# A Toeplitz form cut into 4 KB pieces, and a norm's channel factors moved from the weights to the rows

## The chip, the cores and the metric

One core of a Trainium2 chip runs the whole program in one launch. The metric is device time in microseconds (us); lower is better. The kernel before takes 1645.49 us, the median of three runs (1643.48, 1645.49, 1648.16). The engines are named as in the profile: PE is TensorE (PEld its weight loads), DVE is VectorE, ACT is ScalarE, POOL is GpSimd, SP is SyncE, which issues most of the transfers.

## The reference

Two residual layers over 512 tokens of 1024 channels, all in float32. The even layer mixes tokens with an RWKV-7 recurrence and pooling; the odd layer, where the change lies, with differential attention beside an S5 state-space layer. Both are followed by a mixture of experts (MoE).

```python
h = rms_norm(x, norm_mix_g[layer])          # x * rsqrt(mean(x*x) + eps) * g, g one factor per channel
u = h @ w_in
q, k, v, u_s5 = split(u, ...)               # 512 columns each
...
# S5: 32 groups of 16 channels, a complex diagonal state of 64 per group
bu = einsum('gpc,btgc->btgp', b_bar, uf)
_, states = associative_scan(combine, (lam_bar, bu))
y = einsum('gcp,btgp->btgc', c_mat, states).real + d_skip * uf
```

## The kernel before, in words

The program runs the even mixer, its MoE, the odd mixer and its MoE one after another. A scheduler orders each engine's instructions when the program is built; generators in the source (`run_all`) interleave what it gets. Each engine works its own list strictly in that order, so an instruction that waits holds everything behind it.

**Odd projections.** `odd_mixer` transposes x on PE into eight blocks of 128 channels (`pt`), and splits each into a rounded part and a remainder, `hhi` on ACT and `hlo` on DVE (lines 1817 to 1821). `project(c0, cols)` (line 1869) multiplies them by 512 columns of the weights. A weight ring holds pieces that SP loads; for every pair of channel blocks `split_gain` (line 156) makes `whi` on ACT and `wlo` on DVE, two instructions of 128x512 on each, since each block has its own column of channel factors `gain`. Then come 24 matmuls `pu` (four row blocks, two channel blocks, three products: lines 1883 to 1885), 96 in a unit of 512 columns. There are four units: the S5 input (`to_states`), then keys, queries and values (`to_attention`). After the key and the query unit a chain of ACT and DVE work normalises and rotates the heads (`us`, `rsq`, `sq`, `wk`, lines 1911 to 1936), and PE transposes each result (`ptq`, line 1941).

**The S5 layer** (`states()`, line 1967) works on 64 chunks of 8 tokens. `U` holds the input with 8 tokens times 16 channels on the 128 partitions. What follows, in order:

- `W` (POOL and DVE, lines 1983 to 1985) is transposed on PE (`pw`) to `Wt`, which takes a chunk into the state; `P7` holds the powers of the decay for it.
- `pk` (line 2002) makes the response of the layer, 128 numbers per row (8 lags times 16 channels), 16 rows per group; ACT copies it to `Ks` (line 2008). POOL's queue writes 112 zeros per row (line 1996) and then the 128 numbers (line 2017) to the DRAM scratch `Kd`, 240 numbers per row.
- `pj` (line 2031) takes the chunks into the state, and a scan with its rotations (lines 2037 to 2051) makes `XP`, on DVE and POOL.
- SP reads `Kd` back as `M` (lines 2053 to 2057), the lower triangular Toeplitz matrix of each group: eight transfers, one per token of a chunk, each to 16 partitions in runs of 512 bytes, each shifted by 16 numbers. `M` takes the memory of `Wt`, so the first transfer waits for the last `pj`.
- `pyy` (lines 2063 and 2067) adds `U` times `M` and `XP` times `Q`: 16 groups of matmuls, four of them to a bank, and ACT copies the bank out (line 2070).

PE's list mixes all this with the `pu` matmuls of the attention units. The next stage is attention with the gated unit of the S5 output; the MoE's weights are streamed behind it.

## Time and profile before

| | |
|---|---|
| median of three runs | 1645.49 us |
| the profiled execution | 1643.12 us |
| its span in the trace | 1641.4 us |
| PE busy | 1528.8 us, 93% of the span |
| DVE busy | 819.5 us, 50% |
| ACT busy | 447.9 us, 27% |
| POOL busy | 230.4 us, 14% |
| odd mixer before attention | about 868 to 1021 us of the span |

The shares are means over stages with different limits, so they tell where to look and not what a change is worth. The trace gives for each instruction its start and length, and in brackets the idle time of its engine ahead of it with what ended that. The span is 1.7 us shorter than the execution, and the profiled execution 2.4 us shorter than the median.

### The profile page before, as it was taken

Reading aid. Unit: us, or ns where it says so; the run is one execution under the profiler, and the core shown is the slowest. Engines: PE = TensorE matmul, PEld = TensorE weight load, DVE = VectorE, ACT = ScalarE, POOL = GpSimd, SP = SyncE. Lnnn points to the kernel's source line nnn. Section 1 sums busy time; section 2 is a strip of 40 time slices with the busy share of each in tenths; the row PEclk is TensorE's granted clock in tenths of the full one; section 3 lists DMA queues with packets and bytes.
Section 4 is the critical chain, followed back from the end, with each engine's and each line's share of the span. In section 5 each row is a group of like instructions: output and inputs, shape, how many; then the busy total and the mean of one; then the engine's idle time right before and its main releaser. Section 6 shows DMA issues by size and latency. Waiting matters only on the chain. (4 is left out here: it accounts for less than half of the span.)

```text
span 1641.4 us, 24906 instructions
## 1 busy us (share of the span) xinstructions
PE 1528.8 (93%) x9852; PEld 886.1 (54%) x9852; DVE 819.5 (50%) x1942; ACT 447.9 (27%) x1029; POOL 230.4 (14%) x268
## 2 busy tenths in 40 slices
PE   8998988999999999999998998799999999999997
PEld 6776666776444444433348775577544444433433
DVE  5577878776233333332764694764433333322323
ACT  5234434332212121111314533741021211211110
POOL 2342331200000000000211242501000000000000
PEclk9999999999999999999999999799999999999999
DMA  7210100177899999999992262209789999999996
GB/s 223 97 65 21 51 4 2 53 295 294 337 420 419 419 420 420 420 419 418 420 387 63 66 94 59 103 26 356 308 363 420 419 420 420 419 420 421 420 420 236
DMA packets 95564, 453.62 MB, mean 276 GB/s; under 512 B 12507, under 2 KB 30715, under 8 KB 49360
## 3 DMA queue, kind: packets, MB, share of 16 engines
q1 hardware_dynamic: 88144, 438.01, 67.9%
q0 software_dynamic: 5968, 13.58, 2.4%
q8 instruction: 80, 1.31, 0.3%
q10 hardware_dynamic: 1328, 0.36, 0.1%
q14 instruction: 44, 0.36, 0.1%
HBM read 452.91 MB, written 6.78 MB: 280 GB/s over the span
## 5 line engine op out<-in xcount | busy, mean ns | idle before, releaser
L1198 PE MATMUL pgu<-w,XT 128*64 128x512 f32 x1920 | 452.4, 596 | 22.3 <-DMA w<-in_moe_w_gate 19.1
L1198 PEld LDWEIGHTS pgu<-w,XT 128*64 128x64 f32 x1920 | 141.9, 137 | 312.3 <-issue 256.6
L1288 DVE TENSOR_TENSOR x<-pc,x 128x512 f32<-128x512 f32 x240 | 149.3, 682 | 163.6 <-PE pc L1198 163.6
L1198 PE MATMUL pd<-w,hTe 128*64 128x512 f32 x960 | 213.9, 598 | 0.6 <-ACT hTe L1336 0.6
L1327 DVE SCALAR_TENSOR_TENSOR hid<-hid,gs,pgu 128x512 f32<-128x512 f32 x32 | 23.9, 747 | 242.6 <-PE pgu L1198 234.9
L1095 POOL DMA_INDIRECT rows<-rows,idx x30 | 30.0, 999 | 759.6 <-DVE O L1215 590.3
L1198 PEld LDWEIGHTS pd<-w,hTe 128*64 128x64 f32 x960 | 66.6, 137 | 122.7 <-issue 112.9
L1256 ACT ACTIVATE XT<-pga,p_norm 128x128 f32<-128x128 f32 x240 | 68.3, 371 | 195.1 <-PE pga L1198 191.3
L1345 DVE TENSOR_TENSOR ylo<-pd,yhi 128x512 fp32r<-128x512 f32 (+1 forms) x68 | 44.8, 659 | 138.8 <-ACT yhi L1344 138.8
L1326 ACT ACTIVATE hid<-pgu,gs 128x512 f32<-128x512 f32 x32 | 22.0, 688 | 288.9 <-PE pgu L1198 288.9
L1198 PE MATMUL pc<-yhi,S 128*128 128x512 f32 x240 | 100.4, 418 | 0.0
L1198 PE MATMUL pc<-ylo,S 128*128 128x512 f32 x240 | 94.9, 395 | 0.0
L1344 ACT ACTIVATE yhi<-pd 128x512 fp32r<-128x512 f32 (+1 forms) x68 | 38.9, 572 | 170.9 <-PE pd L1198 153.4
L161 DVE SCALAR_TENSOR_TENSOR wlo<-w,p_norm,whi 128x512 fp32r<-128x512 f32 (+1 forms) x72 | 56.3, 813 | 44.9 <-ACT whi L160 44.9
L160 ACT ACTIVATE whi<-w,p_norm 128x512 fp32r<-128x512 f32 (+1 forms) x72 | 46.3, 692 | 77.8 <-PE pu L665 42.3
L1198 PEld LDWEIGHTS pc<-yhi,S 128*128 128x128 f32 x240 | 45.3, 189 | 34.1 <-issue 26.0
L664 PE MATMUL pu<-hhi,whi 128*128 128x512 f32 x144 | 58.6, 411 | 0.2 <-DVE u L672 0.2
L665 PE MATMUL pu<-hlo,whi 128*128 128x512 f32 x144 | 57.8, 401 | 0.0
L1884 PE MATMUL pu<-wlo,hhi 128*128 128x512 f32 x128 | 53.4, 419 | 3.4 <-DVE wlo L161 3.4
L666 PE MATMUL pu<-hhi,wlo 128*128 128x512 f32 x144 | 55.2, 402 | 0.0
L1883 PE MATMUL pu<-whi,hhi 128*128 128x512 f32 x128 | 51.0, 416 | 1.7 <-ACT us L1895 1.7
L1885 PE MATMUL pu<-whi,hlo 128*128 128x512 f32 x128 | 52.5, 416 | 0.0
(539 smaller groups left out, 2502.7 us busy)
## 6 DMA issues: line engine op xcount, KB each, us to landing
w<-in_moe_w_down SPq DMA_DIRECT2D x120, 1024.0 KB, 20.0
w<-in_moe_w_gate SPq DMA_DIRECT2D x120, 1024.0 KB, 20.0
w<-in_moe_w_up SPq DMA_DIRECT2D x120, 1024.0 KB, 20.2
w<-in_even_w_in SPq DMA_DIRECT2D x8, 1024.0 KB, 5.2
w<-in_moe_w_gate SPq DMA_DIRECT2D x16, 512.0 KB, 8.2
w<-in_moe_w_up SPq DMA_DIRECT2D x16, 512.0 KB, 9.6
w<-in_moe_w_down SPq DMA_DIRECT2D x16, 512.0 KB, 9.3
w<-in_odd_w_in SPq DMA_DIRECT2D x8, 1024.0 KB, 5.1
```

The lines of the kernel that those rows point to most:

```text
L160: nc.scalar.activation(hi[:, k, :], w[:, k, :], AF.Copy, scale=g[:, k:k + 1])
L161: nc.vector.scalar_tensor_tensor(lo[:, k, :], w[:, k, :], g[:, k:k + 1], r32(hi[:, k, :]), op0=OP.mult, op1=OP.subtract)
L664: nc.tensor.matmul(out[j], a, hhi[:, kt, :], start=kt == 0, stop=False)
L665: nc.tensor.matmul(out[j], a, hlo[:, kt, :], start=False, stop=False)
L666: nc.tensor.matmul(out[j], b, hhi[:, kt, :], start=False, stop=kt == KD - 1)
L1198: return self.K.tc.keep_in_program_order(op(*args, **kw))
L1256: nc.scalar.activation(self.XTs[j][:, k, :], p[:, i, :], AF.Copy, scale=B.gain[:, k:k + 1])
L1288: V.tensor_tensor(self.x[:, t, c], p, self.x[:, t, c], OP.add)
L1345: self.nc.vector.tensor_tensor(yl[:, c], p, r32(yh[:, c]), OP.subtract)
L1883: nc.tensor.matmul(out[j], a, whi[:, k, :], start=kt == 0, stop=False)
L1884: nc.tensor.matmul(out[j], a, wlo[:, k, :], start=False, stop=False)
L1885: nc.tensor.matmul(out[j], b, whi[:, k, :], start=False, stop=kt == KD - 1)
```

## The change

Three things change together.

1. `Kd` is laid out anew: the 32 groups split as 4 times 8, and the 8 lie innermost, so that a row has 240 entries of 8 numbers. `M` is then read by four transfers over all 128 partitions, each in one run of 4 KB per partition. For that the tokens of a chunk stand in reverse in `us` and `U`, and the powers `P7` with them. The zeros go out in eight stores in place of one, with the same 512 runs of 448 bytes. ACT writes `Ks` with a step of 8 numbers (32 bytes), and the `pyy` matmuls read `M` with that step.
2. The channel factors of the odd norm multiply the rows when `hhi` and `hlo` are made, and no longer the weights. The weights are split by `split`, one instruction of 128x1024 on each of ACT and DVE in place of two of 128x512.
3. The interleaving counts of `states()` change by one `yield`.

```diff
@@ -1804,7 +1804,8 @@
     lv = cp.tile([128, 6, 64], F32, name="lv")
     A.dma_start(lv.rearrange("p a b -> p (a b)"), I["lam"].to_broadcast([128, 384]))
     K.ocst = K.load(cp, "c_odd", ODD_CONST)
-    Kd = dram.tile([32, 16, 240], F32, name="Kd")
+
+    Kd = dram.tile([4, 16, 240, 8], F32, name="Kd")
     v = []
     qkT = [keep.tile([128, 4, T], F32, name=f"qkT{i}") for i in range(2)]
 
@@ -1818,7 +1819,8 @@
         p = bank("pt")
         for t in range(NT):
             nc.tensor.transpose(p[:, t * 128:(t + 1) * 128], x[:, t, k * 128:(k + 1) * 128], ident)
-        first = split(K, p, hhi[:, k, :], hlo[:, k, :])
+        first = A.activation(hhi[:, k, :], p, AF.Copy, scale=gain[:, k:k + 1]).ins
+        V.scalar_tensor_tensor(hlo[:, k, :], p, gain[:, k:k + 1], r32(hhi[:, k, :]), op0=OP.mult, op1=OP.subtract)
         if k <= PK:
             last = first
 
@@ -1875,7 +1877,7 @@
                 wv = K.ring("o", c0, h // 2)
             whi = K.sp.tile([128, kk, 512], F32R, name="whi", tag="whi")
             wlo = K.sp.tile([128, kk, 512], F32R, name="wlo", tag="wlo")
-            split_gain(K, wv[:, h % 2 * kk:(h % 2 + 1) * kk, :], gain[:, h * kk:(h + 1) * kk], whi, wlo)
+            split(K, wv[:, h % 2 * kk:(h % 2 + 1) * kk, :], whi, wlo)
             for j in range(NT):
                 for k in range(kk):
                     kt = h * kk + k
@@ -1892,13 +1894,13 @@
             yield
         us = st.tile([128, 32, 4, 16], F32, name="us", tag="s5_xp")
         for s in range(4):
-            A.activation(us[:, :, s, :], out[s].rearrange("p (g c) -> p g c", c=16), AF.Copy, scale=rsp[:, s:s + 1])
+            A.activation(us[:, :, 3 - s, :], out[s].rearrange("p (g c) -> p g c", c=16), AF.Copy, scale=rsp[:, s:s + 1])
         yield
         for q in range(4):
             p = bank("pU").rearrange("p (g k) -> p g k", g=8)
             for a in range(8):
                 for hf in range(2):
-                    nc.tensor.matmul(p[H[hf], a, :], us[:, 8 * q + a].rearrange("p s c -> p (s c)"),
+                    nc.tensor.matmul(p[H[1 - hf], a, :], us[:, 8 * q + a].rearrange("p s c -> p (s c)"),
                                      ident[:, hf::2], start=True, stop=True)
             A.activation(U[:, 8 * q:8 * q + 8, :], p, AF.Copy)
             yield
@@ -1971,7 +1973,7 @@
         for r in range(2):
             p7 = st.tile([128, 16, 8], F32, name=f"s5_p7{r}", bufs=1)
             for s in range(8):
-                G.tensor_copy(p7[:, :, s], S.L[:, r, :, 7 - s])
+                G.tensor_copy(p7[:, :, s], S.L[:, r, :, s])
             P7.append(p7[:, :, :, None].to_broadcast([128, 16, 8, 16]))
         Wt = st.tile([128, 32, 128], F32, name="s5_Wt", tag="s5_wm", bufs=1)
         Wt = Wt.rearrange("p (r i) n -> p r i n", r=2)
@@ -1989,11 +1991,13 @@
                     nc.tensor.transpose(p[:, a, :], W[:, a].rearrange("p s c -> p (s c)"), ident)
                 A.activation(Wt[:, r, sl, :], p, AF.Copy)
 
-        Ks = st.tile([128, 2, 4, 128], F32, name="s5_Ks", tag="s5_xp", bufs=1)
+        Ks = st.tile([128, 128, 8], F32, name="s5_Ks", tag="s5_xp", bufs=1)
         G.memset(Ks, 0.0)
         zt = st.tile([16, 112], F32, name="s5_zt", bufs=1)
         G.memset(zt, 0.0)
-        G.dma_start(Kd.rearrange("g c n -> c g n")[:, :, 0:112], zt[:, None, :].to_broadcast([16, 32, 112]))
+        for j in range(8):
+            G.dma_start(Kd[:, :, 14 * j:14 * j + 14, :].rearrange("q c n g -> c q (n g)"),
+                        zt[:, None, :].to_broadcast([16, 4, 112]))
         for h in range(2):
             p = bank("pk").rearrange("p (a n) -> p a n", a=4)
             for i in range(16):
@@ -2005,16 +2009,16 @@
                 if i == 7:
                     yield
             for cg in range(4):
-                A.activation(Ks[32 * cg:32 * cg + 16, h], p[32 * cg:32 * cg + 16], AF.Copy)
+                A.activation(Ks[32 * cg:32 * cg + 16, :, 4 * h:4 * h + 4].rearrange("p n a -> p a n"),
+                             p[32 * cg:32 * cg + 16], AF.Copy)
             yield
         td = st.tile([128, 8, 16], F32, name="s5_td", bufs=1)
         V.tensor_tensor(td, i16[:, None, :].to_broadcast([128, 8, 16]),
                         dsk[:, :, None].to_broadcast([128, 8, 16]), OP.mult)
-        k0 = Ks.rearrange("p h a n -> p (h a) n")[:, :, 0:16]
+        k0 = Ks[:, 0:16].rearrange("p n g -> p g n")
         V.tensor_tensor(k0, k0, td, OP.add)
         for cg in range(4):
-            dst = Kd.rearrange("(ha q) c n -> c ha q n", q=4)[:, :, cg, 112:240]
-            G.dma_start(dst, Ks[32 * cg:32 * cg + 16].rearrange("p h a n -> p (h a) n"))
+            G.dma_start(Kd[cg, :, 112:240, :], Ks[32 * cg:32 * cg + 16])
         yield
 
         XP = st.tile([128, 2, 16, 65], F32, name="s5_XP", tag="s5_xp", bufs=1)
@@ -2050,17 +2054,18 @@
                 G.tensor_tensor(X[1], Y[1 - r], s, OP.mult)
                 V.tensor_tensor(XP[:, r, sl, 1:65], X[0], X[1], OP.add if r else OP.subtract)
                 yield
-        M = st.tile([128, 32, 128], F32, name="s5_M", tag="s5_wm", bufs=1)
-        for s in range(8):
-            src = bass.AP(tensor=Kd.tensor, offset=Kd.offset + (7 - s) * 16,
-                          ap=[[240, 16], [3840, 32], [1, 128]])
-            nc.sync.dma_start(M[16 * s:16 * s + 16], src)
+        M = st.tile([128, 4, 128, 8], F32, name="s5_M", tag="s5_wm", bufs=1)
+        for q in range(4):
+            src = bass.AP(tensor=Kd.tensor, offset=Kd.offset + 30720 * q,
+                          ap=[[128, 8], [1920, 16], [1, 1024]])
+            nc.sync.dma_start(M[:, q].rearrange("p n g -> p (n g)"), src)
+        yield
         for q in range(4):
             p = bank("pyy").rearrange("p (a n) -> p a n", a=4)
             for a in range(4):
                 i = 4 * q + a
                 for h in range(2):
-                    nc.tensor.matmul(p[H[h], a, :], U[:, 16 * h + i, :], M[:, 16 * h + i, :],
+                    nc.tensor.matmul(p[H[h], a, :], U[:, 16 * h + i, :], M[:, i % 4, :, 4 * h + i // 4],
                                      start=True, stop=False)
                 for r in range(2):
                     for h in range(2):
@@ -2077,7 +2082,7 @@
     U = st.tile([128, 32, 64], F32, name="s5_U")
     todo = states()
     run_all((to_states(), 9), (part(todo, SN), SN))
-    run_all((to_attention(), 30), (todo, 24))
+    run_all((to_attention(), 30), (todo, 25))
     dram.release()
     st.release()
     wp.release()
```

The scheduler has ordered the lists anew. Three places matter below. On PE, between the last `pj` and the first `pyy` (a `pu` followed by a number is a bank of `project`). Before:

```order
L1885 MATMUL pu_8578<-whi,hlo 128x512
L1884 MATMUL pu_8579<-wlo,hhi 128x512
L1885 MATMUL pu_8579<-whi,hlo 128x512
L2063 MATMUL pyy<-s_M,s_U 64x128 x2
L2067 MATMUL pyy<-s_Q_6601,s_XP 64x128 x2
```

With the change:

```order
L1885 MATMUL pu_8555<-whi,hhi 128x512
L1885 MATMUL pu_8556<-whi,hhi 128x512
L1885 MATMUL pu_8557<-whi,hhi 128x512
L1885 MATMUL pu_8558<-whi,hhi 128x512
L2068 MATMUL pyy<-s_M,s_U 64x128 x2
L2072 MATMUL pyy<-s_Q_6601,s_XP 64x128 x2
```

Before, 51 `pu` matmuls stand between the last `pj` and the first `pyy`; now 29, the last four of which need `whi` alone. The 47 that follow the first `pyy` up to the first `ptq` of the queries were 32.

On DVE, the rotation of the queries (`us`, `sq`, `wk`) and the splits among it. Before:

```order
L1930 TENSOR_TENSOR us_8370<-us_8370,rsq 128x512
L1934 TENSOR_TENSOR sq<-us_8367,ts_7469 128x8x32 x2
L161 SCALAR_TENSOR_TENSOR wlo<-w,p_norm,whi 128x512
L1936 TENSOR_TENSOR wk<-wk,sq 128x512
L161 SCALAR_TENSOR_TENSOR wlo<-w,p_norm,whi 128x512
L1934 TENSOR_TENSOR sq<-us_8368,ts_7469 128x8x32 x2
```

With the change:

```order
L1932 TENSOR_TENSOR us_8353<-us_8353,rsq 128x512
L1936 TENSOR_TENSOR sq<-us_8350,ts_7469 128x8x32 x2
L1938 TENSOR_TENSOR wk<-wk,sq 128x512
L128 TENSOR_TENSOR wlo<-w,whi 128x1024
L1936 TENSOR_TENSOR sq<-us_8351,ts_7469 128x8x32 x2
```

The first `wk` no longer stands behind a split.

On POOL, the zeros among the products for `W`. Before:

```order
L1983 TENSOR_TENSOR s_W<-s_B,s_p_7560 128x512 x2
L1996 DMA Kd<-s_zt 16x32x112
L1983 TENSOR_TENSOR s_W<-s_B,s_p_7560 128x512 x2
L1983 TENSOR_TENSOR s_W<-s_B,s_p_7569 128x512 x4
L1993 MEMSET s_Ks 128x1024
```

With the change:

```order
L1985 TENSOR_TENSOR s_W<-s_B,s_p_7558 128x512 x2
L1999 DMA Kd<-s_zt 16x4x112 x8
L1985 TENSOR_TENSOR s_W<-s_B,s_p_7558 128x512 x2
L1985 TENSOR_TENSOR s_W<-s_B,s_p_7567 128x512 x4
L1995 MEMSET s_Ks 128x1024
```

Eight issues stand ahead of the third product where one stood. On PE, 47 `pu` matmuls stand ahead of the transpose of that product; before, 6 did.

## Rows read from the trace of the kernel before

**Rows 1.** The page's head.
```profile
span 1641.4 us, 24906 instructions
```

**Rows 2.** Busy time by stretch: first column the stretch, granted clock after POOL.
```profile
core 0: us, PE busy (x) PEld busy (x) DVE busy (x) ACT busy (x) POOL busy (x), PEclk, DMA share, GB/s
960.00:980.00 20.00, 16.63 (x128) 13.45 (x127) 19.58 (x23) 9.74 (x16) 7.80 (x6) 0.93 0.81 93
980.00:1000.00 20.00, 15.63 (x82) 11.15 (x82) 16.61 (x31) 1.93 (x3) 6.34 (x4) 0.73 0.67 93
```

**Rows 3.** PE in order of time: start, length, instruction, idle time before it.
```profile
974.22 1.09 PE L1883 MATMUL pu<-whi,hhi 128*128 128x512 f32 x4
978.68 0.80 PE L1884 MATMUL pu<-wlo,hhi 128*128 128x512 f32 x1 [3.37 <-DVE wlo L161]
...
989.71 0.69 PE L2063 MATMUL pyy<-s_M,s_U 128*64 128x128 f32 x4 [4.37 <-issue]
...
995.50 0.51 PE L1883 MATMUL pu<-whi,hhi 128*128 128x512 f32 x1
...
1003.02 0.60 PE L1941 MATMUL ptq<-idt,wk 128*128 128x128 f32 x4
1003.55 0.44 PE L2063 MATMUL pyy<-s_M,s_U 128*64 128x128 f32 x4
...
1004.51 0.44 PE L2063 MATMUL pyy<-s_M,s_U 128*64 128x128 f32 x4
...
1020.97 1.04 PE L2203 MATMUL pzt<-idt,s_csn 128*128 128x128 f32 x8
```

**Rows 4.** SP's queue in order of time.
```profile
967.26 8.77 SPq L2057 DMA_DIRECT2D s_M<-Kd  x8
```

**Rows 5.** Transfers by line: count, size of one, median time to landing.
```profile
w<-in_odd_w_out SPq DMA_DIRECT2D x4, 1024.0 KB, 4.8
s_M<-Kd SPq DMA_DIRECT2D x8, 256.0 KB, 11.7
Kd<-s_zt POOLq DMA_DIRECT2D x1, 224.0 KB, 4.2
```

**Rows 6.** DVE in order of time.
```profile
945.49 4.71 DVE L1930 TENSOR_TENSOR us<-us,rsq 128x512 f32<-128x512 f32 x4
...
989.02 4.63 DVE L1930 TENSOR_TENSOR us<-us,rsq 128x512 f32<-128x512 f32 x4
993.57 0.75 DVE L1934 TENSOR_TENSOR sq<-us,ts 128x256 f32<-128x256 f32 x2
997.32 0.75 DVE L161 SCALAR_TENSOR_TENSOR wlo<-w,p_norm,whi 128x512 fp32r<-128x512 f32 x1 [3.00 <-ACT whi L160]
997.99 0.68 DVE L1936 TENSOR_TENSOR wk<-wk,sq 128x512 f32<-128x512 f32 x1
```

**Rows 7.** DVE groups by line: busy us, mean ns of one, idle before.
```profile
L161 DVE SCALAR_TENSOR_TENSOR wlo<-w,p_norm,whi 128x512 fp32r<-128x512 f32 x32 | 26.6, 866 | 20.5 <-ACT whi L160 20.4
L2252 DVE TENSOR_TENSOR x<-po,x 128x1024 f32<-128x1024 f32 x4 | 4.9, 1224 | 10.7 <-PE po L2251 10.7
```

**Rows 8.** ACT in order of time, and two ACT groups by line.
```profile
940.75 2.40 ACT L2008 ACTIVATE s_Ks<-pk 16x512 f32<-16x512 f32 x4
...
L2207 ACT ACTIVATE zT<-pzt 128x128 f32<-128x128 f32 x16 | 4.5, 453 | 0.0
L1256 ACT ACTIVATE XT<-pga,p_norm 128x128 f32<-128x128 f32 x240 | 68.3, 371 | 195.1 <-PE pga L1198 191.3 <-issue 3.8
```

**Rows 9.** Weight loads of PE by line.
```profile
L1198 PEld LDWEIGHTS pga<-idt,rows 128*128 128x128 f32 x240 | 32.2, 196 | 30.5 <-issue 22.7 <-DMA rows<-rows,idx 6.0 <-ACT XT L1256 1.8
L1989 PEld LDWEIGHTS pw<-idt,s_W 128*128 128x128 f32 x32 | 3.6, 141 | 2.7 <-ACT s_U L1903 2.2
```

**Rows 10.** POOL in order of time.
```profile
905.03 0.73 POOL L1996 DMA_DIRECT2D Kd<-s_zt  x1
```

**Rows 11.** Who waited for whom on PE, after 1020 us: total, times, longest.
```profile
PE pgu L1198 <- DMA w<-in_moe_w_gate: 9.8, 9, 1.4
```

## The prediction

> **What bounds the kernel now.** The stretch to look at is the odd mixer before attention, and the view to read first is busy time by stretch [rows 2]. Between 960 and 1000 us PE is busy 16.63 and 15.63 of each 20 us, and its granted clock falls to 0.93 and 0.73 of full speed; outside this stretch it is the bound most of the time. PE in order of time tells why [rows 3]: it stands 3.37 us for a `wlo` before 978.68, and 4.37 us before the first `pyy` at 989.71, put down to "issue". No engine releases that one, so a transfer does: `M`, issued from 967.26 on, right behind the last `pj` [rows 4], eight transfers of 256 KB with a median of 11.7 us to landing [rows 5]. From 967.3 to 989.7 it took 22.4 us.
>
> Each wait is paid twice, since PE ran at the lower of its two clock levels (1.2 GHz, not 2.4) after it. The 17 `pu` matmuls from 978.68 on end at 985.34, where the next wait begins: 6.66 us. At full clock a `pu` takes 0.235 (32 of them between 995.50 and 1003.02 [rows 3]), so 17 take 4.0, and 2.7 us are lost. The four `pyy` groups from 989.71 to 995.50 take 5.8 us; at 0.96 a group (1003.55 to 1004.51) they would take 3.8, and 2.0 us are lost. Waits and clock together cost 3.4 + 4.4 + 2.7 + 2.0 = 12.5 us. That is the most that this place can give back.
>
> The second thing to see is DVE. It is busy 19.58 of 20 us from 960 to 980 [rows 2], and its order of time [rows 6] shows a chain that ends only at 998.67: the rotation of the keys starts at 945.49, that of the queries at 989.02, the first `wk` of the queries at 997.99. The first `ptq` of the queries needs that `wk`. PE is late enough today (1003.02) not to notice.
>
> What is won before attention is won at the end: behind it PE waits for the MoE's weights only 9.8 us in nine pieces [rows 11], and those loads start when the odd mixer frees their memory.
>
> **The change, part by part.** Times are those of the profiled execution: span 1641.4 [rows 1], 1.7 less than the execution and 4.1 less than the median of the runs; the sum is a difference, and I set it against the median.
>
> *The transfer of M.* 2 MB in both cases, now in runs of 4 KB over all partitions. The nearest row is the load of the output weights, 1 MB in 4.8 us [rows 5], also 4 KB runs over all partitions: two of those, one after the other, are 9.6 us. The far end is today's 22.4. I take 9.6: all of M is there 9.6 us after the last `pj`. PE comes to its first `pyy` 29 matmuls after the `pj`, 6.8 us, but the four pieces serve the four groups in turn, so that the fourth is wanted 3.4 us later. M is no longer late, or by under 1 us.
>
> *What is late next.* Without waits PE reaches the first `ptq` of the queries 6.8 + 3.8 (four groups) + 47 x 0.235 = 11.0, so 21.6 us after the last `pj`: at 988.9, if `pj` ends at 967.3 as now. DVE is not ready then. Its chain from the start of the keys' rotation to the start of the queries' is 989.02 - 945.49 = 43.5 us, and holds five pairs of `wlo`. A pair costs 2 x 0.866 [rows 7]. In its place comes one 128x1024 subtraction; the nearest row is an addition of that size, 1224 ns [rows 7]. It saves 0.5 us each at best, 2.5 in all, and nothing if POOL's work beside it slows a long instruction more than two short ones; I take 1.7. So the chain takes 41.8 us.
>
> *Its start.* The keys' rotation is preceded on DVE by an addition to `Ks`, so by ACT's copies of `Ks`, two sets of four; the later runs at 940.75 for 2.40 us [rows 8]. They now write with a step of 32 bytes. ACT copies of 128x128 with such a step take 453 ns, without it 371 [rows 8]: 82 ns per 128 numbers, 0.33 per copy of 512, 2.6 us over eight copies. That is the upper end, since copies overlap; the lower end is nothing. I take half, 1.3. The wider `whi` among them, one start in place of two, takes something back; between nothing and all of the 1.3 I take 0.7. The start moves by +0.6, to 946.1.
>
> *The sum.* The queries' rotation starts at 946.1 + 41.8 = 987.9. Four `us` take 4.6, then `sq` 0.7 and `wk` 0.7, now with no split and no 3.00 us wait for `whi` between them: 993.9. From the first `ptq` PE needs what it needed from 1003.02 to 1020.97, 17.95 us, and two more `pu`, 0.5. That ends at 1012.3. Two costs come on top. PE will have stood for up to 5 us (988.9 to 993.9), so a spell at the lower clock follows as after the two waits of today: 2.0 of 2.0 to 2.7, nothing at the lower end if M's lateness fills the gap. And the `pyy` matmuls read `M` with a step of 32 bytes, which no moving operand does in this trace. The nearest row is a weight load with that step, 196 ns against 141 for a contiguous one of the same shape [rows 9]: 55 ns per 128 numbers. In the 12 groups behind the `ptq` there are 48 such passes: 2.6 us if all of it shows, nothing if it hides; I take 1.3, and the first four groups lie in the wait. The end is 1012.3 + 2.0 + 1.3 = 1015.6 against 1020.97 now: **5.4 us gained**, 1640.1 against the median.
>
> The Trainium skill, "SBUF — State Buffer", section "Door 1: The DMA port swizzle", speaks against this layout: SBUF is read in lines of 16 bytes, an access that crosses to a new line pays, and so float32 may be stepped by at most four numbers without cost. The weight loads agree; for a moving operand no row shows it. By that rule the 2.6 us would show in full, and the sum would be 4.1 us.
>
> *The channel factors.* `hhi` and `hlo` get a factor per partition: eight instructions on each engine, under 0.2 us dearer each, at a time when PE has `pu` matmuls in hand; ACT gains as much on each wider `whi`. Nothing, either way; without that cover it would be 1 us.
>
> *The zeros.* Eight issues of up to 0.73 us [rows 10] in place of one put the third product for `W` back by at most 5.1 us on POOL. The 47 `pu` matmuls that now stand ahead of its transpose cover 11.0 us. Nothing; uncovered it would be those 5.1.
>
> **The rivals.**
>
> *The step of 32 bytes costs what it seems to.* All 64 passes exposed, at twice the price of the weight load: 48 x 0.11 = 5.3 us in place of 1.3. For it: each number lies in another 32 bytes. Against it: a float32 matmul takes two passes and may have time to spare. Gain 1.4 us: no change.
>
> *The transfer stays long.* If the reads of one 480 KB scratch and not the short runs set the 22.4 us, the last piece lands at 989.7 as now; PE then has 1.0 (last group) + 11.0 + 18.4 and a low-clock spell of 2.0 ahead of it, 1022.1, and 1.3 for the step: 2.4 us slower, no change. Against it: 2 MB in 22.4 us are 94 GB/s, and the load's 1 MB in 4.8 us are 218. In between lies no loss: up to 5 us of lateness are DVE's wait anyway. The Trainium skill, "DMA: Bandwidth & Descriptors", section "Why a DMA increments its semaphore by 16 and not by 1", says that the slowest dimension of both sides sets how many of 16 engines work, and here it is 8 on the DRAM side: half of them, so that M would land later than by the row. No row here shows it; it would make this rival likelier.
>
> *DVE is not late.* If DVE's saving is larger or the start earlier, PE runs through: 988.9 + 18.4 + 1.3 = 1008.6, a gain of 12.4 us.
>
> *POOL is held by its stores* (the slower side). If each small store keeps POOL until it lands, as one took 4.2 us to do [rows 5], eight hold it from 905.0 to 938.6. The third product, its subtraction and the transpose then come at about 942, where PE arrives at about 922: 20 us, of which the gain takes back 5.4: some 14 slower. It decides from about 1.6 us per store (13 us of cover over eight). Against it: the one store released POOL after 0.73.
>
> *Another order in attention.* The lists there changed too, with scores put behind the gate's matmuls. Two waits with their low clock, about 6 us, could come or go; that widens the range on both sides.
>
> **How the numbers follow.** About 0.3%, 4.9 us, is what a measurement of this kernel can tell from no change. Chances: the forecast 0.46, the dear step 0.16, the long transfer 0.12, DVE not late 0.14, POOL held 0.04, attention worse by 6 us 0.08. The forecast alone lies between 2 and 10 us gained. It is close to the 4.9, so I count 0.34 of its 0.46 as faster, all 0.14 of DVE not late and 0.03 of the rest: 0.51 faster. Slower are POOL held, 0.04 of attention and 0.03 of the long transfer with costs at their upper ends: 0.11. The rest, 0.38, is no change. The predicted time is 1640.0 us. The range reaches from 1631 (DVE not late, and the step free) to 1649 (the long transfer, 1647.9, with a part of the dear step).
>
> **What would show it.** Right: `M` lands within 13 us of the last `pj`, the wait before the first `pyy` is under 2 us, `wlo` appears as 128x1024 at 1.2 to 1.7 us, and a new wait of PE stands before the first `ptq` of the queries, ended by DVE's `wk`. Wrong: `pyy` matmuls on `M` with starts well over 0.1 us apart, a PE wait for `s_W` of more than 2 us near 920, or a wait before `pyy` as long as today's; and if PE does not wait at that `ptq`, the chain on DVE was not what is late next.

## The result, and the profile after

The changed kernel takes 1653.72 us, the median of six runs (1652.24 to 1655.16), against 1643.82 us for the kernel before, run beside it: the ratio is 1.0057, with a 95% interval of 1.0042 to 1.0072. It is slower by 9.9 us. The forecast was 1640.0 and the range 1631 to 1649; the measured time lies above both, and the change lost where a gain was forecast.

Of the two profiled executions, the span grew from 1641.4 to 1651.8 us. Measured from the first transpose of x (`pt`) to the first `pzt`, the odd stage before attention grew from 152.0 us (869.0 to 1021.0) to 158.0 (870.5 to 1028.5). These 6.0 us are what the change can be seen to do. The other 4.4 lie upstream (1.5) and in the last MoE (3.0; the parts are rounded), in places that it leaves alone; the last section comes back to them.

The view that answers to [rows 2], busy time by stretch of the kernel after (its columns: the stretch, its length, busy time of each engine and instructions in brackets, PE's granted clock, DMA share, GB/s):

```profile
960.00:980.00 20.00, 20.00 (x176) 16.22 (x176) 18.25 (x24) 9.95 (x15) 8.90 (x7) 0.98 0.30 91
980.00:1000.00 20.00, 11.53 (x63) 7.26 (x60) 18.18 (x29) 0.61 (x2) 8.58 (x5) 0.66 0.56 120
```

The hole is not gone but comes later, and is deeper: PE is busy 11.53 of 20 us from 980 on, at 0.66 of full clock. The view that answers to [rows 3, 4], PE and SP's queue in order of time (start, length, instruction, idle time ahead of it and what ended that):

```profile
955.07 0.79 PE L1886 MATMUL pu<-wlo,hhi 128*128 128x512 f32 x1 [4.77 <-DVE wlo L128]
...
972.98 2.63 SPq L2061 DMA_DIRECT2D s_M<-Kd  x4
...
984.03 0.66 PE L2068 MATMUL pyy<-s_M,s_U 128*64 128x128 f32 x4 [3.01 <-DMA s_M<-Kd]
989.88 0.71 PE L2068 MATMUL pyy<-s_M,s_U 128*64 128x128 f32 x4 [4.16 <-DMA s_M<-Kd]
994.09 0.71 PE L2068 MATMUL pyy<-s_M,s_U 128*64 128x128 f32 x4 [1.30 <-DMA s_M<-Kd]
...
1007.49 0.60 PE L1943 MATMUL ptq<-idt,wk 128*128 128x128 f32 x4
```

Three things are to be seen. First, the four pieces of M are issued within 2.6 us from 972.98 on, but PE waits for the second, third and fourth, 8.5 us in all; the fourth is there at 994.09. From the first issue that is 21.1 us, where the old form took 22.4: the new form brought next to nothing. (From 980.44 on, a load of 1 MB for the output weights runs beside it, as one does in the kernel before from 979.32 on.) Secondly, there is a new wait of 4.77 us for a `wlo` long before M, at 955. Where it comes from stands on ACT and DVE; the old copies of `Ks` took 2.40 us for four [rows 8], and the keys' rotation began at 945.49 [rows 6]:

```profile
940.88 4.77 ACT L2012 ACTIVATE s_Ks<-pk 16x512 f32<-16x512 f32 x4
...
945.75 0.46 DVE L2019 TENSOR_TENSOR s_Ks<-s_Ks,s_td 128x128 f32<-128x128 f32 x1 [2.66 <-ACT s_Ks L2012]
...
948.56 4.65 DVE L1932 TENSOR_TENSOR us<-us,rsq 128x512 f32<-128x512 f32 x4
953.13 0.74 DVE L1936 TENSOR_TENSOR sq<-us,ts 128x256 f32<-128x256 f32 x2
953.80 1.21 DVE L128 TENSOR_TENSOR wlo<-w,whi 128x1024 fp32r<-128x1024 f32 x1
```

ACT's copies take twice as long, DVE waits 2.66 us for them with its small `Ks` addition, everything behind that in DVE's list comes later for it, and the `wlo` that PE wants stands behind the four rotations. Thirdly, each group of `pyy` matmuls on M now takes longer. The group of the kernel before (the numbers are the shortest, median and longest record):

```profile
L2063 PE MATMUL pyy<-s_M,s_U x64: 272/323/474, 989.7 to 1014.8; 128*64 128x128 f32 x64
```

The same group after:

```profile
L2068 PE MATMUL pyy<-s_M,s_U x64: 411/417/477, 979.8 to 1021.8; 128*64 128x128 f32 x64
```

### The profile page after: what moved, and what is told of

Its sections match the earlier page's. It is cut to its first block, busy times and chain, and to the rows that moved or that the text cites. A ratio compares the mean times of both kernels' runs of the same rounds, so it can differ in the third digit from the quotient of the medians.

```text
span 1651.8 us, 24879 instructions
## 1 busy us (share of the span) xinstructions
PE 1534.3 (93%) x9852; PEld 886.0 (54%) x9852; DVE 819.1 (50%) x1926; ACT 448.8 (27%) x1013; POOL 236.0 (14%) x275
## 5 line engine op out<-in xcount | busy, mean ns | idle before, releaser
L1198 PEld LDWEIGHTS pc<-ylo,S 128*128 128x128 f32 x240 | 45.2, 188 | 8.2
L1198 PEld LDWEIGHTS pga<-idt,rows 128*128 128x128 f32 x240 | 32.2, 196 | 31.3 <-issue 22.7
```

What stands on the lines that cost most here:

```text
L1198: return self.K.tc.keep_in_program_order(op(*args, **kw))
```

## The experiments

Four questions were open: which half of the change costs, what holds the transfer of M, what the 32-byte steps cost on ACT and on PE, and whether a version beats both kernels.

### The halves

`e1_gain_only` is the kernel before with the factors on the rows, `e2_toeplitz_only` the changed kernel without them, its one further `yield` kept. The edit of the first is shown, without its line for `hlo`; the second turns the same lines back:

```diff
-        first = split(K, p, hhi[:, k, :], hlo[:, k, :])
+        first = A.activation(hhi[:, k, :], p, AF.Copy, scale=gain[:, k:k + 1]).ins
...
-            split_gain(K, wv[:, h % 2 * kk:(h % 2 + 1) * kk, :], gain[:, h * kk:(h + 1) * kk], whi, wlo)
+            split(K, wv[:, h % 2 * kk:(h % 2 + 1) * kk, :], whi, wlo)
```

> The kernel before with the odd norm's factors on the rows and unsplit wide weight splits, the Toeplitz parts as they were. Theory A (the Toeplitz part is what costs, the factors are a small gain): 1639 to 1644 us against 1643.8, with the queue wait for wlo ahead of the last pu smaller than the 3.4 us of before. Rival B (the factors cost through a new order of the scheduler): 1646 us or more, with new waits on TensorE before the M matmuls.

> The changed kernel with the norm's factors back in the weight splits of 128x512. Theory A (the Toeplitz part costs all of the 9.9 us and more): 1653 to 1658 us, the four M pieces again 4 to 5 us apart, ACT copies of Ks 4.7 us in a group of four, M matmuls in 1.17 us a group. Rival B: under 1648 us, if the two parts only cost together.

The factors alone: 1644.78 us, ratio 1.0000 (0.9985 to 1.0015). The wait for `wlo` is 3.1 us where it was 3.4, and the wait for M 5.8 us where it was 4.4. The Toeplitz half alone: 1653.11 us, ratio 1.0058 (1.0041 to 1.0075). The Toeplitz half, with the `yield`, is the whole loss, and the factors are worth nothing that can be told from no change.

### The copies of Ks

`e7_ks_order` leaves every byte where the change puts it. ACT only walks the tile in another order:

```diff
-                A.activation(Ks[32 * cg:32 * cg + 16, :, 4 * h:4 * h + 4].rearrange("p n a -> p a n"),
-                             p[32 * cg:32 * cg + 16], AF.Copy)
+                A.activation(Ks[32 * cg:32 * cg + 16, :, 4 * h:4 * h + 4],
+                             p[32 * cg:32 * cg + 16].rearrange("p a n -> p n a"), AF.Copy)
```

> The changed kernel; the eight copies of Ks on ScalarE walk the tile in its memory order (four floats in a row, then a step of 32 bytes) and read PSUM with a step of 512 bytes. Theory A (single floats written at 32-byte steps are the price): the groups of four take 2.4 to 3.2 us where the change takes 4.7, the wait of 4.8 us for wlo at 955 us is under 3 us, and 1649 to 1652 us. Theory B (any step on either side costs the same): 4.4 us or more per four and 1653 us or more.

It takes 1645.79 us, ratio 1.0005 (0.9991 to 1.0019): 7.9 us better than the change, more than either theory said. ACT and DVE in order of time, in this run:

```profile
938.63 2.40 ACT L2012 ACTIVATE s_Ks<-pk 16x512 f32<-16x512 f32 x4
...
941.13 0.41 DVE L2019 TENSOR_TENSOR s_Ks<-s_Ks,s_td 128x128 f32<-128x128 f32 x1 [0.30 <-ACT s_Ks L2012]
...
943.90 4.71 DVE L1932 TENSOR_TENSOR us<-us,rsq 128x512 f32<-128x512 f32 x4
```

The copies are back at 2.4 us per four, the step now being on the side that ACT reads, `pk` in PSUM, the memory that PE writes its results to. The rotation starts 4.7 us earlier, the 4.77 us wait for `wlo` is gone, and with it the spell at the lower clock behind it (0.50 from 956 to 960 us in the change, 1.00 here). The last `pj` starts at 965.5 and not at 972.7, and the stage takes 150.8 us, 7.2 less. The waits for M are those of the change, 8.7 us there too. So 4.65 us of ACT time, in two sets of copies, cost over 7 us on PE.

### What holds the transfer of M

`e3_m_sixteen` reads M with 16 as the slowest index, eight transfers of 16 partitions:

```diff
-        for q in range(4):
-            src = bass.AP(tensor=Kd.tensor, offset=Kd.offset + 30720 * q,
-                          ap=[[128, 8], [1920, 16], [1, 1024]])
-            nc.sync.dma_start(M[:, q].rearrange("p n g -> p (n g)"), src)
+        for s in range(8):
+            src = bass.AP(tensor=Kd.tensor, offset=Kd.offset + 128 * s,
+                          ap=[[1920, 16], [30720, 4], [1, 1024]])
+            nc.sync.dma_start(M[16 * s:16 * s + 16].rearrange("p q n g -> p q (n g)"), src)
```

`e4_m_apart`, `e5_m_plain` and `e10_c_outer` keep the change's four transfers and alter only where they read, `e12_m_near` does so with those of `e3_m_sixteen`, and `e11_old_spread` gives the kernel before, with its 512-byte runs, transfers over all 128 partitions. All of these but `e3_m_sixteen` fill M with other numbers than the kernel wants, and each of them was run once, so that their rates and waits count and not their times:

```diff
e4
-            src = bass.AP(tensor=Kd.tensor, offset=Kd.offset + 30720 * q,
-                          ap=[[128, 8], [1920, 16], [1, 1024]])
+            src = bass.AP(tensor=I["moe_w_gate"].tensor, offset=135680 * q,
+                          ap=[[16896, 8], [1024, 16], [1, 1024]])
e5
-                          ap=[[128, 8], [1920, 16], [1, 1024]])
+                          ap=[[232, 128], [1, 1024]])
e10
-                          ap=[[128, 8], [1920, 16], [1, 1024]])
+                          ap=[[1920, 16], [128, 8], [1, 1024]])
e12
-                          ap=[[1920, 16], [30720, 4], [1, 1024]])
+                          ap=[[232, 16], [30720, 4], [1, 1024]])
e11
-                          ap=[[240, 16], [3840, 32], [1, 128]])
-            nc.sync.dma_start(M[16 * s:16 * s + 16], src)
+                          ap=[[16, 128], [3840, 8], [1, 128]])
+            nc.sync.dma_start(M[:, 8 * q:8 * q + 8], src)
```

> The changed kernel; M is read by eight transfers of 16 partitions x 4 runs of 4 KB, so that the slowest index of both sides counts 16 and not 8. Theory A (the outer index of 8 puts a transfer on half of the 16 DMA engines, which the DMA share of 0.5 in 973 to 994 us shows): share near 1, all of M there within 11 to 13 us of the first issue where the change takes 21, the 8.5 us of waits for M under 3 us, and 1646 to 1650 us. Theory B (reads that overlap in one 480 KB stretch of DRAM set the rate): 18 us or more again, 1652 us or more.

> The changed kernel; its four M transfers keep their shape (8 x 16 runs of 4 KB into 128 partitions, 512 KB each), but read runs that lie apart in a large weight tensor in place of runs that overlap in the 480 KB scratch, so M holds weights and the output is not the reference's. TensorE's order is that of the change. Theory A (all reads falling on one small, overlapping stretch of DRAM set the 105 GB/s): M is all there within 12 us of the first issue, the 8.5 us of waits for M are under 2 us, and the profiled span is 4 us or more shorter. Theory B (the shape of the transfer, 8 as slowest index, or 4 KB runs): 18 us or more again, waits of 7 us or more.

> The changed kernel; the four M transfers read 128 runs of 4 KB with a single step (928 B) inside the same scratch stretch, so the slowest index is 128 and not 8, and M holds other elements of the scratch (the output is not the reference's). Theory A (the small overlapping stretch sets the rate): all 16 engines busy, yet again 17 us or more for the 2 MB. Theory B (the shape): 12 us or less.

> The changed kernel; the four M transfers read the same runs of the same scratch, with the 16 channels as slowest index and the 8 shifts inside (16 x 8 for 8 x 16), so neighbouring partitions hold other rows than TensorE wants and the output is not the reference's. TensorE's order is the change's. Theory A (what matters is over how many partitions the engines write at the same moment; 8 x 16 and eight transfers of 16 partitions both write 16 neighbours or 8 partitions 16 apart): over 200 GB/s in 973 to 985 us, all of M there within 12 us of the first issue, waits for M under 2 us, span 4 to 8 us under the change's 1651.8. Theory B (the overlapping rows, 512 B apart, are slow in DRAM wherever they go): 18 us or more again and waits of 7 us or more.

> The kernel before with its scratch layout and runs of 512 B, M read by four transfers over all 128 partitions (128 x 8 runs) in place of eight over 16 partitions (16 x 32 runs); M holds other elements of the scratch, so the output is not the reference's. Theory A (16 partitions at a time hold the old transfer at 100 GB/s, not its 512 B runs): 180 GB/s or more, M there within 13 us of the first issue, the 4.4 us wait before the first M matmul under 1 us. Theory B (512 B runs are the limit): 20 us or more again.

> The run with eight M transfers of 16 partitions x 4 runs of 4 KB, with rows 928 B apart in the scratch in place of 7680 B (the step of the run with 128 rows that moved 363 GB/s); the output is not the reference's. Theory A (16 destination partitions at a time are the limit): 115 to 130 GB/s and 18 us or more again, a wait of 5 to 7 us before the first M matmul. Theory B (the rows' distance in DRAM): over 200 GB/s and no wait.

Busy time by stretch again, where the last two numbers are the share of the 16 DMA engines and GB/s. Four us of the kernel before, with its eight transfers of 16 neighbouring partitions:

```profile
970.00:974.00 4.00, 4.00 (x19) 3.21 (x19) 3.90 (x6) 2.24 (x4) 1.18 (x1) 1.00 1.28 105
```

The change, 8 x 16 runs of 4 KB per transfer:

```profile
974.00:978.00 4.00, 4.00 (x19) 3.26 (x18) 3.90 (x7) 2.02 (x3) 1.30 (x1) 1.00 0.46 128
```

`e3_m_sixteen`, 16 neighbouring partitions with runs of 4 KB:

```profile
978.00:982.00 4.00, 3.38 (x15) 2.46 (x14) 4.00 (x4) 1.06 (x1) 3.22 (x2) 1.00 1.05 121
```

`e12_m_near`, the same with rows 928 bytes apart in DRAM:

```profile
978.00:982.00 4.00, 4.00 (x19) 3.23 (x18) 4.00 (x5) 0.00 (x1) 1.13 (x2) 1.00 1.06 121
```

`e10_c_outer`, 16 x 8 runs over all partitions:

```profile
978.00:982.00 4.00, 4.00 (x26) 2.65 (x26) 4.00 (x6) 1.06 (x1) 3.06 (x2) 1.00 1.01 244
```

`e5_m_plain`, 128 runs with one step:

```profile
974.00:978.00 4.00, 4.00 (x19) 3.26 (x18) 3.90 (x6) 1.79 (x3) 1.38 (x2) 1.00 0.98 363
```

`e11_old_spread`, 128 partitions with runs of 512 bytes:

```profile
970.00:974.00 4.00, 4.00 (x19) 3.24 (x18) 3.90 (x6) 2.79 (x5) 1.31 (x1) 1.00 1.19 307
```

- The change keeps half of the engines busy (0.46). With all of them (1.05) `e3_m_sixteen` moves no more, 121 GB/s, and PE waits 6.5 us. Its theory A is refuted: that all engines work does not bring M in time. It does not clear the count of engines in the change, though, since this edit also narrows what is written at a time to 16 neighbours. The run still takes 1646.77 us, 7 less than the change; its list on PE is another one, its stage gives 2.1 of that, and of the profiled execution's 7.3 us the last MoE, which the edit leaves alone, has 4.5. So this gain is not explained by M.
- `e5_m_plain` reads overlapping rows of the same 480 KB scratch at 363 GB/s. PE waits for M no more, and does wait 3.23 us at the first `ptq`, for DVE's `wk`:

```profile
998.66 1.09 PE L1943 MATMUL ptq<-idt,wk 128*128 128x128 f32 x4 [3.23 <-DVE wk L1938]
```

Its theory A, the rival of the prediction, is refuted too: the small scratch alone does not hold the rate.

- `e11_old_spread` moves 307 GB/s with the old runs of 512 bytes, and the wait before the first `pyy` is gone; the profiled execution's span is 1636.9 us. The run length was not what held M.
- `e12_m_near` has the row distance of `e5_m_plain` and the 16 partitions of `e3_m_sixteen`, and is as slow as the latter: its theory A.
- `e10_c_outer` has all of M there 11.6 us after the first issue; the waits for M are 0.4 us and the span 1646.1: its theory A. But against the change it has all engines at work, and at a time they serve other partitions and other rows, so it does not say which of the three doubled the rate.
- `e4_m_apart` lies between its theories: the waits for M are 5.8 us, and the last one ends 15.1 us after the first issue. Engines and destination are those of the change, so where the runs are read counts for something in the form of 8 x 16, too. At the start the two are alike (124 and 128 GB/s from 974 to 978); later they are not. The change from 988 to 992 us:

```profile
988.00:992.00 4.00, 2.12 (x13) 1.45 (x14) 3.86 (x10) 0.00 (x0) 1.59 (x1) 0.50 0.52 124
```

And `e4_m_apart`:

```profile
988.00:992.00 4.00, 3.69 (x21) 1.97 (x22) 3.89 (x9) 0.00 (x0) 1.79 (x1) 0.54 0.51 198
```

As an estimate from `e5_m_plain`, half of its engines would move half of 363, some 181 GB/s. With the same eight engines and the same partitions `e4_m_apart` gets there, and the change does not.

### The same bytes, with the rows apart

What the old form and `e3_m_sixteen` have in common is where a transfer writes. `e13_old_rows` is the kernel before with the rows of a chunk in another order, half, channel, token, so that each of the eight transfers with its 512-byte runs writes 16 partitions that lie 4 apart and not 16 neighbours:

```diff
-        us = st.tile([128, 32, 4, 16], F32, name="us", tag="s5_xp")
+        us = st.tile([128, 32, 16, 4], F32, name="us", tag="s5_xp")
...
-            nc.sync.dma_start(M[16 * s:16 * s + 16], src)
+            nc.sync.dma_start(M[64 * (s // 4) + s % 4:64 * (s // 4) + 64:4], src)
```

`us`, `U`, `W` and `Wt` follow in the same order. `e9_both` is the changed kernel with the copies of `e7_ks_order` and the transfers of `e3_m_sixteen`, and `e14_new_rows` is that with the new row order.

> The changed kernel with both repairs: Ks copied in the tile's memory order, M read by eight transfers of 16 partitions; its order on TensorE is that of the run with the M transfers alone. Theory A (the two losses add): the copies save the wait of 4.8 us for wlo here too, 1638 to 1642 us, below the kernel before. Rival B (with M as late, an earlier issue is all that is won): 1643 to 1646 us.

> The kernel before, its scratch, runs of 512 B and copies untouched; only the rows of the chunk (U, Wt, M) are put in the order half, channel, token, so each of the eight M transfers writes 16 partitions that lie 4 apart in place of 16 neighbours. Theory A (neighbouring destination partitions hold a transfer to 100 to 125 GB/s, partitions 4 apart do not): over 180 GB/s, all of M there within 14 us of the first issue, the wait of 4.4 us before the first M matmul under 1 us, and 1637 to 1642 us against 1644.5. Theory B (any transfer into 16 partitions is slow, or the 512 B runs hold it): 20 us or more again, a wait of 3 us or more, 1643 to 1648 us.

> The changed kernel with Ks copied in the tile's memory order, rows of the chunk in the order half, channel, token, and M read by eight transfers of 16 partitions 4 apart x 4 runs of 4 KB. Theory A: over 180 GB/s, the 6.3 us wait for M of the run with both repairs under 1.5 us, and 1636 to 1640 us, 2 to 5 us under that run's 1641.5. Theory B (16 partitions, whatever their distance): 115 to 125 GB/s, a wait of 5 us or more, 1640 to 1644 us. The 64 M matmuls keep their 32-byte step, so by theory A it stays within 2 us of the kernel before with the same row order, to either side.

Busy time by stretch of `e9_both`, 16 neighbouring partitions:

```profile
974.00:978.00 4.00, 3.68 (x16) 2.63 (x14) 3.97 (x5) 0.75 (x1) 1.65 (x1) 1.00 1.05 120
```

`e14_new_rows`, the same runs into 16 partitions 4 apart:

```profile
974.00:978.00 4.00, 2.49 (x12) 1.99 (x11) 4.00 (x4) 0.22 (x1) 2.67 (x2) 1.00 1.06 213
```

`e13_old_rows`, 16 partitions 4 apart with the old 512-byte runs:

```profile
974.00:978.00 4.00, 2.67 (x12) 1.83 (x10) 3.79 (x6) 1.33 (x2) 2.25 (x2) 1.00 1.26 165
```

With the same reads, 16 partitions at a time in both cases and the same engines, 120 GB/s become 213 when the partitions lie apart; and 105 become 155 to 165 with the old short runs, under the 180 that theory A asked for. The wait for M is gone in both. This shows the cause for transfers into 16 partitions, the old form among them. For the change's own 8 x 16 it is not shown. The times are 1641.50 us for `e9_both` (ratio 0.9977, 0.9964 to 0.9989), 1640.33 for `e14_new_rows` (0.9971, 0.9957 to 0.9984) and 1635.66 for `e13_old_rows`, ratio 0.9948 (0.9933 to 0.9963). All three beat both kernels, and the one that does without the new layout does so by most. `e14_new_rows` loses the 6.3 us wait of `e9_both` and yet comes out only 1.2 us lower, inside the intervals, where 2 to 5 us were expected: a wait for `wlo`, which M's lateness had covered, now stands at the end of the same stretch:

```profile
993.55 0.80 PE L1886 MATMUL pu<-wlo,hhi 128*128 128x512 f32 x1 [2.17 <-DVE wlo L128]
```

It is also 4.7 us above `e13_old_rows`, and not within the 2 us expected; the stages of the two profiled executions show 1.4 of that (147.7 against 146.3), and the rest is not explained.

The Trainium skill, "SBUF — State Buffer", section "Door 1: The DMA port swizzle", has the rule: partitions reach 16 ports in a fixed pattern, 16 neighbours reach four of them, and the page gives 104 GB/s for that. The runs agree, with 105 to 121. By its pattern, 16 partitions 4 apart in one half reach eight ports; the 155 to 213 GB/s go that way. Eight partitions 16 apart, which the change writes if its eight engines keep step, reach only four by the pattern; that they keep step no run shows, and the 198 GB/s of `e4_m_apart` into the same partitions speak against four ports as the whole of the change's 128.

### The step on PE, and the factors once more

`e6_contig` has PE read neighbours in M, other numbers than it wants, with every list as in the change. `e15_rows_and_gain` is `e13_old_rows` with the factors on the rows.

```diff
-                    nc.tensor.matmul(p[H[h], a, :], U[:, 16 * h + i, :], M[:, i % 4, :, 4 * h + i // 4],
+                    nc.tensor.matmul(p[H[h], a, :], U[:, 16 * h + i, :], M[:, i % 4, 16 * (4 * h + i // 4):16 * (4 * h + i // 4) + 16].rearrange("p n g -> p (n g)"),
```

> The changed kernel; the 64 M matmuls read 128 neighbouring elements of M in place of every eighth (the wrong elements, so the output is not the reference's); the order on every engine is the change's. Theory A (TensorE pays for the 32-byte step of its moving operand): groups of four matmuls start 0.37 us apart where the change has 0.59, and with 12 of 16 groups after the last of wk 2.6 us less: 1650 to 1652 us. Theory B (the step is free, the 411 ns records are the wait for a clock or a weight load): no change, 1653 to 1655 us.

> The run with the old scratch and the rows in the order half, channel, token, and beside it the change's other part: the odd norm's factors on the rows and unsplit wide weight splits. Theory A (the factors gave nothing alone because TensorE then waited for M anyway; with M in time the shorter splits show): 1632 to 1634 us against that run's 1635.7, with the wait of 3.4 us for wlo near 980 shorter. Theory B (the splits are not on the path, the wait for wlo has ACT's whi behind it): within 1.5 us of 1635.7, the wait for wlo still 3 us or more.

`e6_contig` takes 1650.21 us (1.0026, 1.0012 to 1.0040), 3.5 less than the change, and its stage is 3.5 shorter. The stage is the better witness: the six times lie in two groups, near 1648 and near 1652.4, with the median between them. PE in order of time in the change:

```profile
1008.02 0.66 PE L2068 MATMUL pyy<-s_M,s_U 128*64 128x128 f32 x4
1008.61 0.65 PE L2072 MATMUL pyy<-s_Q,s_XP 64*64 64x128 f32 x8
1009.19 0.66 PE L2068 MATMUL pyy<-s_M,s_U 128*64 128x128 f32 x4
```

And in `e6_contig`:

```profile
1008.41 0.44 PE L2068 MATMUL pyy<-s_M,s_U 128*64 128x128 f32 x4
1008.78 0.65 PE L2072 MATMUL pyy<-s_Q,s_XP 64*64 64x128 f32 x8
1009.36 0.44 PE L2068 MATMUL pyy<-s_M,s_U 128*64 128x128 f32 x4
```

Four records take 0.59 us with the step and 0.37 without, which is theory A; over 64 records that is 3.5 us, 55 ns each. `e15_rows_and_gain` takes 1637.87 us (0.9958, 0.9942 to 0.9973), no better than without the factors, and the wait for `wlo` is still 3.5 us: theory B, though the difference of 2.2 us is a little over its bound and inside the intervals.

## Why the prediction was wrong

- **"I take 9.6: all of M is there 9.6 us after the last pj."** This step failed: it took 21.1 from the first issue. The row it rests on, the output weights in 4.8 us per MB [rows 5], is like M in run length and count of partitions, and I took the run length for the cause. The old transfer was held by its 16 neighbouring partitions, not by its runs. The new one keeps half of the engines busy, and late in the transfer it moved 124 GB/s where rows apart let the same engines move 198; how much falls to the engines, to the rows and to the partitions written at a time stays open. The rival of the long transfer came true, but its reason is at most a part: the same scratch was read at 363 GB/s, though rows apart saved 6.0 of the 21.1 us. The sentence beside it, that a slowest index of 8 means half the engines (the Trainium skill, "DMA: Bandwidth & Descriptors", section "Why a DMA increments its semaphore by 16 and not by 1"), agrees with the share of 0.46. All the engines moved no more into 16 neighbours and nearly twice as much over all partitions.
- **"I take half, 1.3", and the start "moves by +0.6".** This failed worst, since no rival carried it. The copies cost 4.65 us more, some 2.3 for each set of four; the row of 453 against 371 ns [rows 8] was of another shape and far too kind. The start moved by 3.1 us, to 948.56 (1.5 of them come from upstream; against `e7_ks_order`, which differs in the copies alone, it is 4.7). The place where that hurt was not the chain to `wk` but the `wlo` behind it, wanted by PE: 4.77 us and a low-clock spell. I looked only at the far end of DVE's list.
- **"I take 1.3" for the strided pyy matmuls.** A mis-sized term: the upper end was right. 12 groups by 0.22 us are 2.6 us, 55 ns per pass as the weight load had shown [rows 9], all of it exposed, and 3.5 over all 16 groups. The rule of the Trainium skill that was set against this step held for this operand. Its four numbers without cost did not hold for ACT's writes, as the last section has it.
- **DVE's saving, "I take 1.7".** It came in part, and a new wait covered it. The chain from rotation to rotation took 43.95 us (948.56 to 992.51) where it was 43.5, and in it DVE stands for PE's `ptq`, which comes late behind the late `wlo`; in the kernel before it does not:

```profile
961.43 0.76 DVE L1936 TENSOR_TENSOR sq<-us,ts 128x256 f32<-128x256 f32 x2 [3.09 <-PE ptq L1943]
```

In `e7_ks_order`, without that wait, the chain takes 41.95 us, near the 41.8 forecast; the queries' rotation there:

```profile
985.85 4.66 DVE L1932 TENSOR_TENSOR us<-us,rsq 128x512 f32<-128x512 f32 x4
```

The new splits alone give 42.42 us (`e1_gain_only`), 1.1 less than before. The new order with the old splits gives 42.52 (`e2_toeplitz_only`), so the 41.95 is not the splits' work alone. That `e1_gain_only` and `e15_rows_and_gain` are no faster says that the saving is not on PE's path there.

- **"What is late next"** was right in kind, and seen only once M was in time: in `e5_m_plain` PE stands 3.23 us at the first `ptq`, ended by DVE's `wk`, 26 us behind the last `pj`; the forecast gave 26.6. That the two are so near is luck: the `pj` and the `ptq` both come some 5 us later than forecast.
- **The factors and the zeros: nothing.** Right. POOL's eight issues took 4.17 us at 906.20, with no wait for `W` behind them.
- **The bound of 12.5 us** was not contradicted: with M in time, and nothing else changed, the stage gives back 7.6 us (`e11_old_spread`, 152.0 to 144.4).
- **Slower**: POOL was not held, and attention from the first `pzt` to the MoE's first `pgu` took 139.0 us, before 139.1. The long transfer came, but not at its price: in `e7_ks_order`, with M as late as in the change and the step at its full cost, the stage is 1.2 us shorter than before, where the rival had 2.4 more, and the time is that of the kernel before (1.0005). So M's lateness and the step took away the gain, and the copies made a loss of it.
- **With both failed steps mended** (`e14_new_rows`) the stage takes 147.7 us, 4.3 less than before. The sum gave 5.4, or 4.1 with the step at its full price. So near a hit is in part luck, since the row order made ACT's writes of `us` dearer and the wait for `wlo` at 993.55 was not foreseen.

## What to carry to other kernels

Before a transfer is given longer runs, find out whether the runs hold it. Probes that read other data are cheap, but each should change one thing only of run length, engines, source and destination; those that changed two or three here left the new form's own rate unexplained. Into 16 partitions, the destination alone was worth 50 to 93 GB/s. A step that a layout asks of the other engines has to be priced on the engine that writes it and on the one that reads it, in their own shape. And what a delay costs is read from the next instruction behind it that somebody waits for, not from the end of the chain.

## What was not expected of the hardware

- In these runs ACT paid for a step on the side it writes. A 16x512 copy took 588 ns with neighbours written, 1164 with a step of 32 bytes, and 590 when it wrote four neighbours at a time and read PSUM with a step of 512 bytes. In `e13_old_rows` its 128x512 writes of `us` with a step of 16 bytes took 1158 ns where the old ones took 678.
- The last MoE, which the change leaves alone, takes 479 to 484 us from its first `pgu` to the end of the span, in no order that follows the kernels; the first `pt` comes at 868.6 to 871.8 us, in no such order either. At one place in the MoE PE waits for a gather of rows, and in some executions its clock stays low behind that. PE in order of time in the change:

```profile
1196.83 1.12 PE L1198 MATMUL pga<-idt,rows 128*128 128x128 f32 x4 [2.69 <-DMA rows<-rows,idx]
```

The same place in the kernel before:

```profile
1189.04 1.12 PE L1198 MATMUL pga<-idt,rows 128*128 128x128 f32 x4 [2.30 <-DMA rows<-rows,idx]
```

And in `e3_m_sixteen`:

```profile
1192.83 0.71 PE L1198 MATMUL pga<-idt,rows 128*128 128x128 f32 x4 [1.54 <-DMA rows<-rows,idx]
```

Four transposes take 1.12, 1.12 and 0.71 us at a granted clock of 0.50, 0.50 and 1.00, and the 32 `pd` matmuls behind them 8.23, 8.40 and 7.09. The kernel before has the spell as well, so it does not explain the 3.0 us between the two. One profile of each kernel can't show how much of the 9.9 us lies in such scatter; the part that the odd stage does not explain stays open.
